# Seven block products for gate and up of the last 1024 tokens, in a one-core transformer layer

## The chip, the core and the metric

One NeuronCore of one Trainium2 chip runs the whole layer in one launch. The metric is device time in microseconds (us), the median of several executions. Engines are named as in the profile: PE is TensorE (PEld its weight loads), DVE is VectorE, ACT is ScalarE, POOL is GpSimd, SP is SyncE, whose queue issues all DMAs of this kernel.

## What is computed

One layer over 2048 tokens of 1024 features: three attention-like mixers, an output projection, then a gated feed-forward network with 2816 hidden features. The change touches the last of these:

```python
x = x + jnp.concatenate([out_a, out_b, out_c], axis=-1) @ w_out[l]
h = rms_norm(x, norm_ffn[l])
x = x + (jax.nn.silu(h @ w_ffn_gate[l]) * (h @ w_ffn_up[l])) @ w_ffn_down[l]
return rms_norm(x, final_norm)
```

All is float32. The kernel keeps each operand as a high part `hi` (the value rounded to fp32r) and a low part `lo = x - hi`, and makes each product of three matmuls: hi·hi, lo·hi and hi·lo.

## The kernel before

Tokens lie along the free axis in four groups of 512. A *tile* is 128 partitions by 512 float32. The program has two stages.

The **merged stage** runs two threads against each other (`merge`): the dense one (input projections, the two linear mixers, then the feed-forward network of token groups 0 and 1, one group at a time) and the sparse attention of all 16 query blocks. It lasts to the end of the last attention block. Weights are split into `hi` and `lo` once there (`load_halves`: ACT makes `hi`, L116, POOL makes `lo`, L119) and stored to DRAM as 512 KB tiles of both halves.

The **last stage** is `ffn([2, 3], ...)` for the last 1024 tokens, as two halves of 512. It loads the 512 KB tiles back (L131) and has these parts:

- The output projection: 8 output tiles times 2 halves times 8 contraction tiles times 3 matmuls (L175 to L177), with a residual add and squares for the norm. `n_lead = 6` output tiles start on contraction tiles 2 to 7 (`others`), since tiles 0 and 1 (`sparse`) come from the sparse attention.
- `normed(i)` per half: one matmul with ones (L202), rstd on ACT (L148, L149), then per contraction tile the scaled token tile on DVE (L229), `hi` on ACT (L231) and `lo` on DVE or POOL in turn (L232).
- For each pair of hidden tiles f, f+1: `gate_up(f)` and `gate_up(f + 1)` (L175 to L177; tanh on ACT L277, products on DVE L278 and L283, split on ACT and POOL L116, L119), then `down` of the pair before (L299 to L302).
- The tail: `down` of the last pair, norm, scaling, output (L326, L329).

The order is that of a scheduler which places the recorded instructions on each engine; a tile's buffers come free with the last use of the tile that held them. The pools of the last stage lie over the memory of those before, so that a load into them can wait for an older tile's last reader.

Of the kernel before, what the change touches and what calls it, by code (L numbers as in the profile page):

```python
# [75 lines left out]
SPEED = 1.3  # L76
FINE = 4

N_RAW, N_W, N_ACT = 3, 5, 3
A_RAW, A_W = 3, 5  # L80
N_GEN, N_MIX, N_ATT, N_NEAR = 4, 3, 3, 2

# [2 lines left out]
def hybrid_encoder_kernel(ctx, tc, xT, w_in, w_out, w_g, w_u, w_d, vec, wuk, wuv, wg2,  # L85
# [18 lines left out]
    cs = const.tile([P, C_SWA], F32, name="cs")  # L104
    vc = const.tile([P, NV], F32, name="vc")
    nc.sync.dma_start(out=vc, in_=vec)
    ident = cs[:, C_ID:C_ID + P]
# [34 lines left out]
    def store_halves():  # L142
        dst, w = unstored.pop(0)
        nc.sync.dma_start(out=dst, in_=w.bitcast(F32))

    def rstd_of(ss, n, dst):
# [10 lines left out]
        A.activation(dst, dst, AF.Exp)  # L157


    def ffn(groups, pools, ps_f, ps_n, n_raw, n_w, n_act, n_lead, before):  # L160

        fx, ft, fh, fl, fo, fs, fr = pools
        nh = len(groups)
        W = nh * 512
        halves = [slice(i * 512, (i + 1) * 512) for i in range(nh)]

        def load_w(src, f, c):
# [13 lines left out]

        sparse, others = range(2), range(2, KC)

        def operand(i, k):
            pool = fo if k in others else fs
            return (pool.tile([P, 512], F32R, tag=f"ah{k}{i}", bufs=1, name="ah"),
                    pool.tile([P, 512], F32R, tag=f"al{k}{i}", bufs=1, name="al"))

        def square(hs, k):

            if k == 0:
                A.activation(rs[:, hs], x2[:, k, hs], AF.Square)
            else:
                sq = fr.tile([P, 512], F32, tag="m", bufs=3, name="sq")
# [11 lines left out]

        def mixed(i, k):
            hi, lo = mixo[i][k]
            m = fr.tile([P, 512], F32, tag="m", bufs=3, name="m")
# [10 lines left out]
        def normed(i):  # L220

            hs = halves[i]
            norm_scale(hs)
            h2.append([])
            for k in range(KC):
                h2[i].append(operand(i, k))
                hi, lo = h2[i][k]
                hf = fr.tile([P, 512], F32, tag="m", bufs=3, name="hf")
# [4 lines left out]
                yield 0.4  # L233

        for k in others:
            mixed(0, k)
# [3 lines left out]
        for i, hs in enumerate(halves):  # L240
            lead = []
            for oc in range(KC):
                w = [load_w(w_out, oc, c) for c in range(2)]
                ps = ps_f()
                yield from product(ps, w, mixo[i], others, last=False)
                lead.append((oc, ps, w))
                yield 3.9 - 0.65 * (KC - FINE)
                if i == 0 and oc < n_lead - 1:
                    continue
                if i == 0 and oc == n_lead - 1:  # L250
                    yield from before
# [12 lines left out]
            yield from normed(i)  # L264

        def gate_up(f):
            ah = ft.tile([P, W], F32R, tag="fh", bufs=n_act, name="fh")
# [4 lines left out]
            for i, hs in enumerate(halves):  # L272
# [4 lines left out]
                A.activation(s, pg, AF.Tanh, scale=0.5)  # L277
                V.scalar_tensor_tensor(out=s, in0=s, scalar=1.0, in1=pg, op0=ALU.add, op1=ALU.mult)  # L278
                yield 5.2 - 0.65 * (KC - FINE)
                pu = ps_f()  # L280
# [4 lines left out]
                yield 5.2 - 0.65 * (KC - FINE)  # L285

        def down(fs, parts, last=False):

            n, ws = len(fs), {}
            for i2, hs in parts:  # L290
                if i2 not in ws:
                    ws[i2] = [load_w(w_d, f, i2) for f in fs]
# [58 lines left out]
    with ExitStack() as mx:  # L351
# [45 lines left out]
        def big():  # L397
            return bigp.tile([P, S], F32, tag="big", name="big")

        wuk_s = const.tile([P, 4, P], F32, name="wuk_s")  # L400
        wuv_s = const.tile([P, 256], F32, name="wuv_s")
        bits = const.tile([P, 32], I32, name="bits")

        def constants():
            nc.sync.dma_start(out=cs, in_=cst[:, 0:C_SWA])
# [713 lines left out]
        def dense():  # L1119
# [9 lines left out]
            with ExitStack() as f1:  # L1129
                fo, fr, fw, fx, ft = [f1.enter_context(tc.tile_pool(name=n, bufs=2))  # L1130
                                      for n in ("f1o", "f1r", "f1w", "f1x", "f1t")]
                pools = fx, ft, fw, fw, fo, fo, fr
                mf = f1.enter_context(tc.tile_pool(name="mf", bufs=3, space=PSUM))
                end = iter(())
                for g in range(2):
                    while len(attended) < 4 * g + 4:
                        yield None
                    end = yield from ffn([g], pools, lambda: mf.tile([P, 512], F32, tag="mf", name="mf"), ps_tr,
                                         N_RAW, N_W, N_ACT, 2, end)
                yield from end  # L1140

        drive(merge((dense(), NG * (PASS1 + PASS2) + 2 * FFN1),
# [1 line left out]

    with ExitStack() as f2:

        fx, ft, fo, fr, fh, fs, fl = [f2.enter_context(tc.tile_pool(name=n, bufs=2))
                                      for n in ("f2x", "f2t", "f2o", "f2r", "f2h", "f2s", "f2l")]
        pools = fx, ft, fh, fl, fo, fs, fr
# [98 lines left out]
```

## Time and profile before

| | us |
|---|---|
| runs | 2954.04, 2942.41, 2954.8; median 2954.04 |
| profiled execution, its own time | 2950.48 |
| its span | 2948.7 |
| merged stage, to the first matmul of the last stage | 2103.6 |
| output projection of the last 1024 tokens | to about 2201.5 |
| gate, up and down of 11 pairs | to about 2915 |
| end | 2948.7 |

The span is what the instruction rows cover; the execution's own time has 1.8 us more around it. The granted TensorE clock, as a mean over the span, is 0.973 of full speed. In rows of the timeline, a column in brackets is the engine's idle time just before, and what released it; `x12` means that so many instructions were put together.

### The profile page before, as it was taken

The numbers are of one execution on the slowest core, as the hardware profiler recorded it, in microseconds if no ns is written. First come the engines' busy times: TensorE is split into PE (matmuls) and PEld (weight loads), VectorE is DVE, ScalarE is ACT, GpSimd is POOL, SyncE is SP. The second block draws the span as 40 slices with busy tenths as digits, with TensorE's granted clock in tenths as the row PEclk, the third lists the DMA queues.
The fourth block names the chain that finished last, engine by engine and source line by source line (L and its number), as shares of the span: only waits on it lengthen the run. The fifth ranks groups of instructions, "written<-read, shape, count | busy, mean of one in ns | idle before, by whom it ended". The sixth has DMA issues, their size and how long they took to land.

```text
span 2948.7 us, 36635 instructions
## 1 busy us (share of the span) xinstructions
PE 2761.6 (94%) x13372; PEld 2171.4 (74%) x13372; DVE 1677.2 (57%) x3567; ACT 1181.1 (40%) x2061; POOL 582.8 (20%) x497
## 2 busy tenths in 40 slices
PE   7898999999999899999989999999899999999997
PEld 5666767676776767777767777777677888888886
DVE  3787887788767867475576673673342222222226
ACT  4655664665546655354553431441341000000004
POOL 3113420010100544444431100001111000000002
PEclk9998999999999989999999999999999999999998
DMA  7665534243332756666655444444572323323222
GB/s 248 193 190 191 183 122 142 92 149 106 103 128 78 268 179 229 227 214 225 226 187 193 142 150 143 137 152 147 188 249 87 108 92 100 100 86 107 93 93 72
DMA packets 179300, 451.12 MB, mean 153 GB/s; under 512 B 18632, under 2 KB 50288, under 8 KB 179120
## 3 DMA queue, kind: packets, MB, share of 16 engines
q1 hardware_dynamic: 179120, 448.78, 46.1%
q8 instruction: 105, 1.72, 0.2%
q14 instruction: 75, 0.61, 0.1%
HBM read 325.88 MB, written 122.83 MB: 152 GB/s over the span
## 4 chain that ended last, share of the span: by engine, by line
PE 59%; DVE 19%; ACT 8%; issue 7%; DMA 4%; POOL 2%; SPq 0%; DVEq 0%; ACTq 0%; POOLq 0%
PE pf L175 6%; PE pf L177 6%; PE pf L176 6%; DVE jd L937 6%; ACT jd L935 4%; PE mf L177 4%; PE mf L175 4%; PE mf L176 4%; PE pf L301 2%; PE pf L300 2%; PE pf L299 2%; PE mm L507 2%; PE mm L506 2%; PE mm L508 2%; PE mf L299 2%
## 5 line engine op out<-in xcount | busy, mean ns | idle before, releaser
L935 ACT ACTIVATE jd<-x,c 128x384 bf16<-128x384 f32 (+13 forms) x224 | 292.8, 1307 | 288.5 <-DVE c L962 228.7
L177 PE MATMUL mf<-al,w 128*128 128x512 f32 x832 | 329.1, 396 | 8.3 <-DVE al L212 4.1
L175 PE MATMUL mf<-ah,w 128*128 128x512 f32 x832 | 331.5, 399 | 3.7 <-ACT ah L231 2.8
L937 DVE TENSOR_SCALAR_CACHE_REDUCE jd<-x,c 128x384 bf16<-128x384 f32 (+13 forms) x224 | 330.9, 1477 | 6.5 <-DVE c L946 0.5
L175 PE MATMUL pf<-ah,w 128*128 128x512 f32 x832 | 325.1, 391 | 6.2 <-DMA w<-w 4.5
L119 POOL TENSOR_TENSOR w<-raw,w 128x512 fp32r<-128x512 f32 x192 | 260.0, 1362 | 341.4 <-ACT w L116 297.0
L176 PE MATMUL mf<-ah,w 128*128 128x512 f32 x832 | 327.4, 395 | 0.0
L177 PE MATMUL pf<-al,w 128*128 128x512 f32 x832 | 324.8, 391 | 1.3 <-POOL al L212 0.6
L176 PE MATMUL pf<-ah,w 128*128 128x512 f32 x832 | 325.3, 391 | 0.0
L119 POOL TENSOR_TENSOR fl<-u,fh 128x512 fp32r<-128x512 f32 x88 | 114.2, 1298 | 948.5 <-ACT fh L116 948.4
L506 PE MATMUL mm<-hh,w 128*128 128x512 f32 x576 | 241.3, 419 | 4.3 <-issue 2.0
L507 PE MATMUL mm<-hh,w 128*128 128x512 f32 x576 | 232.2, 403 | 0.6 <-POOL w L119 0.6
L508 PE MATMUL mm<-hl,w 128*128 128x512 f32 x576 | 230.9, 401 | 0.0
L177 PEld LDWEIGHTS mf<-al,w 128*128 128x128 f32 x832 | 158.5, 191 | 46.4 <-DVE al L212 4.5
L175 PEld LDWEIGHTS mf<-ah,w 128*128 128x128 f32 x832 | 159.0, 191 | 38.4 <-ACT ah L231 3.4
L175 PEld LDWEIGHTS pf<-ah,w 128*128 128x128 f32 x832 | 156.9, 189 | 39.9 <-DMA w<-w 4.9
L302 DVE TENSOR_TENSOR x<-x,pf 128x512 f32<-128x512 f32 (+1 forms) x184 | 121.9, 663 | 110.3 <-PE pf L301 110.0
L177 PEld LDWEIGHTS pf<-al,w 128*128 128x128 f32 x832 | 156.8, 188 | 35.9 <-POOL al L212 1.0
L176 PEld LDWEIGHTS mf<-ah,w 128*128 128x128 f32 x832 | 158.5, 190 | 31.7
L176 PEld LDWEIGHTS pf<-ah,w 128*128 128x128 f32 x832 | 156.8, 188 | 32.8 <-issue 0.5
L116 ACT CAST fh<-u 128x512 fp32r<-128x512 f32 x88 | 54.6, 620 | 308.1 <-DVE u L283 307.6
L299 PE MATMUL mf<-fh,w 128*128 128x512 f32 x352 | 147.0, 418 | 32.7 <-DVE x L302 17.3
(256 smaller groups left out, 5473.1 us busy)
## 6 DMA issues: line engine op xcount, KB each, us to landing
w<-w SPq DMA_DIRECT2D x636, 512.0 KB, 3.5
xk<-in_xT_dram SPq DMA_DIRECT2D x64, 256.0 KB, 3.3
raw<-in_w_in_dram SPq DMA_DIRECT2D x44, 256.0 KB, 3.7
raw<-in_w_g_dram SPq DMA_DIRECT2D x44, 256.0 KB, 3.7
raw<-in_w_u_dram SPq DMA_DIRECT2D x44, 256.0 KB, 3.9
raw<-in_w_d_dram SPq DMA_DIRECT2D x44, 256.0 KB, 4.3
m<-mixT SPq DMA_DIRECT2D x32, 256.0 KB, 3.1
x<-in_xT_dram SPq DMA_DIRECT2D x32, 256.0 KB, 4.6
```

Source lines behind the costliest of these rows:

```text
L119: Q.tensor_sub(lo, src, hi.bitcast(F32))
L175: T.matmul(ps, a, act[k][0], start=(first and k == ks[0]), stop=False)
L176: T.matmul(ps, b, act[k][0], start=False, stop=False)
L177: T.matmul(ps, a, act[k][1], start=False, stop=(last and k == ks[-1]))
L299: T.matmul(ps, hi[:, os_], ah[:, hs], start=(j == 0), stop=False)
L300: T.matmul(ps, lo[:, os_], ah[:, hs], start=False, stop=False)
L302: V.tensor_add(x2[:, oc, hs], x2[:, oc, hs], ps)
L506: T.matmul(ps, a, hh, start=(k == 0), stop=False)
L507: T.matmul(ps, b, hh, start=False, stop=False)
L508: T.matmul(ps, a, hl, start=False, stop=(k == KC - 1))
L935: A.activation(jd, xs, AF.Sign, scale=-1.0, bias=c[:, 0:1], accum_out=cnt)
L937: V.tensor_scalar(out=jd, in0=xs, scalar1=c[:, 0:1], scalar2=0.0, op0=ALU.is_ge, op1=ALU.add, accum_out=cnt)
```

## The change

Gate and up of the last 1024 tokens are cut into blocks: 2 hidden tiles (f, f+1), 2 halves of the contraction (4 tiles each), 2 halves of the tokens. Eight block products of 12 matmuls become seven, of sums of weight blocks (`s1` to `s4`) with sums of token blocks (`t1` to `t4`), as in Winograd's form of Strassen's scheme:

- `second_halves` makes the token sums, in the place of `normed` for the second half; `first_halves` keeps the scaled tiles of the first half (`kept`) for it.
- `quad` runs seven products of one weight matrix for one pair and puts them together on DVE, `take_gate` and `take_up` finish them. `first_quads` does gate and up of pair 0 while the token sums are made: six products run side by side, one contraction tile at a time.
- `summed` loads four raw weight blocks (L151, 256 KB each) and makes four sums on POOL (L153 to L156), `split` makes their halves on ACT and POOL (L114, L117). For pair 0 this runs in the merged stage (`summed_halves`, called from `gate_up` of group 1) and the halves go to DRAM; for the ten later pairs it runs in the last stage, one side ahead (`in_order`, `next_w`).
- The weight buffers of the last stage go from 9 to 6, temporaries from 3 to 7, raw tiles from 3 to 4 (in the merged stage too). Its pools are ordered anew, and four constants leave `const` for `pers`, which makes room.
- Per pair the order is gate, `down` of the pair before, up, where it was gate/up of f, gate/up of f+1, `down`.

```diff
-N_RAW, N_W, N_ACT = 3, 5, 3
+N_RAW, N_W, N_ACT = 4, 5, 3
...
+    def summed(src, f, pool, n_raw):
+        a = {}
+        for r in range(2):
+            for i in range(2):
+                a[r, i] = pool.tile([P, 512], F32, tag="raw", bufs=n_raw, name="raw")
+                nc.sync.dma_start(out=a[r, i], in_=src[f + r][:, i * 512:(i + 1) * 512])
+        s1, s2, s3, s4 = a[1, 1], a[0, 0], a[1, 0], a[0, 1]
+        Q.tensor_add(s1, a[1, 0], a[1, 1])
+        Q.tensor_sub(s3, a[0, 0], a[1, 0])
+        Q.tensor_sub(s2, s1, a[0, 0])
+        Q.tensor_sub(s4, a[0, 1], s2)
...
+        def second_halves():
+            norm_scale(halves[1])
+            for k in range(4):
+                b12, b22, t1, t2, t3, t4 = (temp() for _ in range(6))
+                scaled(k, 1, b12)
+                scaled(k + 4, 1, b22)
+                V.tensor_sub(t1, b12, kept[k])
+                hb["t1"].append(both(16 + k, t1, Q))
+                V.tensor_sub(t2, b22, t1)
+                hb["t2"].append(both(24 + k, t2, V))
+                V.tensor_sub(t3, b22, b12)
+                hb["t3"].append(both(8 + k, t3, Q))
+                V.tensor_sub(t4, kept[k + 4], t2)
+                hb["t4"].append(both(20 + k, t4, Q))
+                hb["b22"].append(both(12 + k, b22, V))
+                yield
...
+        def seventh(w, b):
+            ps = ps_f()
+            for k in range(4):
+                part(ps, w, hb[b][k], k, k == 0, k == 3)
+            return ps
...
         for f in range(0, NF, 2):
-            yield from gate_up(f)
-            if f and n_act < 4:
+            if nh == 1:
+                yield from gate_up(f)
+                if f:
+                    yield from down([f - 2, f - 1], steps)
+                yield from gate_up(f + 1)
+            elif f == 0:
+                yield from first_quads()
+            else:
+                yield from quad(w_g, f, take_gate)
                 yield from down([f - 2, f - 1], steps)
-            yield from gate_up(f + 1)
-            if f and n_act >= 4:
-                yield from down([f - 2, f - 1], steps)
+                room(f)
+                yield from quad(w_u, f, take_up)
...
-        fx, ft, fo, fr, fh, fs, fl = [f2.enter_context(tc.tile_pool(name=n, bufs=2))
-                                      for n in ("f2x", "f2t", "f2o", "f2r", "f2h", "f2s", "f2l")]
+        fx, ft, fs, fo, fr, fh, fb = [f2.enter_context(tc.tile_pool(name=n, bufs=2))
+                                      for n in ("f2x", "f2t", "f2s", "f2o", "f2r", "f2h", "f2b")]
...
-                                 lambda: pr.tile([P, 512], F32, tag="pm", name="pm"), 3, 9, 4, 6, iter(()))
+                                 lambda: pr.tile([P, 512], F32, tag="pm", name="pm"), 4, 6, 4, 6, iter(()))
```

Where instructions come to stand, at three places. First SP's queue at the seam of the two stages, before (`m` are mixer outputs for the projection, `out_dram` is the output of group 1, `w` the weight tiles, `mixT3<-ma` the last attention result):

```order
L210 DMA m_18214<-mixT2_60 128x512
L210 DMA m_18218<-mixT2_60 128x512
L210 DMA m_18222<-mixT2_60 128x512
L329 DMA out_0_dram<-x2_14013 128x2x512 x4
L131 DMA w_18238<-w44_9098 128x1024
L210 DMA m_18226<-mixT2_60 128x512
L210 DMA m_18230<-mixT2_60 128x512
L1088 DMA mixT3_61<-ma_18144 128x2x128
L210 DMA m_18234<-mixT2_60 128x512
L131 DMA w_18240<-w45_9104 128x1024
```

and now, behind seven `m` loads and four `raw` loads that stand just ahead of this piece:

```order
L129 DMA w_18302<-w44_9098 128x1024
L129 DMA w_18304<-w45_9104 128x1024
L129 DMA w_18325<-w46_9132 128x1024
L129 DMA w_18327<-w47_9139 128x1024
L539 DMA out_0_dram<-x2_14013 128x2x512 x4
L129 DMA w_18348<-w48_9221 128x1024
L129 DMA w_18350<-w49_9228 128x1024
L241 DMA m_18446<-mixT2_60 128x512
L247 DMA x2_18441<-in_xT_dram 128x512
L1306 DMA mixT3_61<-ma_18208 128x2x128
L247 DMA x2_18441<-in_xT_dram 128x512 x4
L129 DMA w_18371<-w50_9271 128x1024
```

The first four weight tiles now stand ahead of the output of group 1, and the first of them no longer waits for that output to land; the seventh weight tile waits for one of six buffers.

Second PE's queue where the second half's norm begins, before (`pm` is the matmul with ones, `pf_18934` the first gate product):

```order
L177 MATMUL pf_18934<-al_18567,w_18926 128x512
L175 MATMUL pf_18934<-ah_18572,w_18926 128x512
L202 MATMUL pm_18872<-rs_18376,ones_85 128x512
L176 MATMUL pf_18934<-ah_18572,w_18926 128x512
L177 MATMUL pf_18934<-al_18573,w_18926 128x512
```

and now (`pf_18956` is the second block product, `pf_19013` the third):

```order
L353 MATMUL pf_18956<-ah_18638,w_18954 128x512
L354 MATMUL pf_18956<-al_18639,w_18954 128x512
L233 MATMUL pm_18974<-rs_18440,ones_84 128x512
L352 MATMUL pf_19013<-ah_18644,w_19011 128x512
L353 MATMUL pf_19013<-ah_18644,w_19011 128x512
```

`pm` stood behind 10 matmuls of the stretch that follows the output projection; it stands behind 24 now. Behind it come 24 more that need the first half alone, and then 72 that need token sums.

Third DVE's queue in the same stretch, before (`hf` are scaled tiles, `al` low parts, `s` is a gate):

```order
L229 SCALAR_TENSOR_TENSOR hf_18878<-x2_18377,vc_83,rs_18376 128x512
L229 SCALAR_TENSOR_TENSOR hf_18884<-x2_18377,vc_83,rs_18376 128x512
L229 SCALAR_TENSOR_TENSOR hf_18890<-x2_18377,vc_83,rs_18376 128x512
L229 SCALAR_TENSOR_TENSOR hf_18896<-x2_18377,vc_83,rs_18376 128x512
L232 TENSOR_TENSOR al_18883<-hf_18884,ah_18882 128x512
L229 SCALAR_TENSOR_TENSOR hf_18902<-x2_18377,vc_83,rs_18376 128x512
L278 SCALAR_TENSOR_TENSOR s_18959<-s_18959,pf_18934 128x512
```

and now, for the first of four contraction tiles (`t_18980` to `t_18983` are `t1` to `t4`):

```order
L271 SCALAR_TENSOR_TENSOR t_18978<-x2_18441,vc_82,rs_18440 128x512
L271 SCALAR_TENSOR_TENSOR t_18979<-x2_18441,vc_82,rs_18440 128x512
L300 TENSOR_TENSOR t_18980<-t_18978,hf_18618 128x512
L302 TENSOR_TENSOR t_18981<-t_18979,t_18980 128x512
L304 TENSOR_TENSOR t_18982<-t_18979,t_18978 128x512
L306 TENSOR_TENSOR t_18983<-hf_18642,t_18981 128x512
L277 TENSOR_TENSOR al_18993<-t_18981,ah_18992 128x512
L277 TENSOR_TENSOR al_19007<-t_18979,ah_19006 128x512
```

Twelve DVE instructions for the second half become 32, eight per contraction tile; POOL has three low parts per tile beside them, 12 where it had four.

## Rows read from the trace of the kernel before

**Rows 1.** The page: busy time of the engines, and slices of the span.
```profile
span 2948.7 us, 36635 instructions
...
PE 2761.6 (94%) x13372; PEld 2171.4 (74%) x13372; DVE 1677.2 (57%) x3567; ACT 1181.1 (40%) x2061; POOL 582.8 (20%) x497
...
PE   7898999999999899999989999999899999999997
...
PEclk9998999999999989999999999999999999999998
```

**Rows 2.** Busy time by stretch: us, busy of each engine, clock, DMA share, GB/s.
```profile
1600.00:2080.00 480.00, 454.86 (x2248) 366.25 (x2247) 272.85 (x501) 165.75 (x220) 39.83 (x37) 0.98 0.44 141
2103.00:2204.00 101.00, 94.19 (x397) 75.91 (x398) 37.34 (x51) 27.88 (x43) 15.34 (x11) 0.97 0.82 282
2300.00:2900.00 600.00, 600.00 (x2649) 496.99 (x2648) 154.77 (x226) 43.91 (x72) 46.48 (x36) 1.00 0.29 94
```

**Rows 3.** The page's costliest groups: block matmuls (L176, L177 have as many).
```profile
L175 PE MATMUL pf<-ah,w 128*128 128x512 f32 x832 | 325.1, 391 | 6.2 <-DMA w<-w 4.5
```

**Rows 4.** The timeline of PE at the seam of the stages.
```profile
2103.57 0.47 PE L175 MATMUL pf<-ah,w 128*128 128x512 f32 x1 [1.03 <-DVE ma L1087]
...
2109.71 0.80 PE L175 MATMUL pf<-ah,w 128*128 128x512 f32 x1 [4.52 <-DMA w<-w]
...
2114.97 0.39 PE L175 MATMUL pf<-ah,w 128*128 128x512 f32 x1
```

**Rows 5.** The timeline of SP's queue at the seam.
```profile
2090.80 5.05 SPq L329 DMA_DIRECT2D out_dram<-x  x4
2099.50 0.34 SPq L131 DMA_DIRECT2D w<-w  x1
...
2104.67 18.98 SPq L131 DMA_DIRECT2D w<-w  x11
```

**Rows 6.** Busy time by stretch, after PE's idle time at the seam.
```profile
2110.00:2115.00 5.00, 5.00 (x13) 3.91 (x13) 0.00 (x0) 0.00 (x0) 0.00 (x0) 0.51 1.02 419
2115.00:2120.00 5.00, 5.00 (x24) 4.14 (x23) 0.00 (x0) 0.00 (x0) 0.00 (x0) 1.00 0.83 329
```

**Rows 7.** The timeline of the second half's norm, PE and DVE.
```profile
2203.74 1.12 PE L202 MATMUL pm<-rs,ones 128*128 128x512 f32 x2
...
2207.57 2.08 DVE L229 SCALAR_TENSOR_TENSOR hf<-x,vc,rs 128x512 f32<-128x512 f32 x3 [3.89 <-ACT rs L149]
...
2219.34 1.18 DVE L232 TENSOR_TENSOR al<-hf,ah 128x512 fp32r<-128x512 f32 x1
```

**Rows 8.** One line's instructions: ns min/median/max, of DVE and POOL.
```profile
L229 DVE SCALAR_TENSOR_TENSOR hf<-x,vc,rs x32: 739/746/1781, 1040.3 to 2217.5; 128x512 f32<-128x512 f32 x32
L232 DVE TENSOR_TENSOR al<-hf,ah x16: 675/680/1753, 1045.2 to 2219.3; 128x512 fp32r<-128x512 f32 x16
```

**Rows 9.** Groups by line and shape: operations on POOL, DVE and ACT.
```profile
L119 POOL TENSOR_TENSOR fl<-u,fh 128x512 fp32r<-128x512 f32 x88 | 114.2, 1298 | 948.5 <-ACT fh L116 948.4
L302 DVE TENSOR_TENSOR x<-x,pf 128x512 f32<-128x512 f32 x168 | 115.5, 687 | 109.4 <-PE pf L301 109.1
L116 ACT CAST fh<-u 128x512 fp32r<-128x512 f32 x88 | 54.6, 620 | 308.1 <-DVE u L283 307.6
```

**Rows 10.** The page's DMA issues: KB each, us from issue to landing.
```profile
w<-w SPq DMA_DIRECT2D x636, 512.0 KB, 3.5
raw<-in_w_u_dram SPq DMA_DIRECT2D x44, 256.0 KB, 3.9
```

**Rows 11.** What PE waited for: first 2195 to 2230 us, last row 2230 to the end.
```profile
PE pf L175 <- ACT ah L231: 0.7, 1, 0.7
PE pf L177 <- DVE al L232: 0.5, 1, 0.5
PE pf L177 <- POOL al L232: 0.2, 1, 0.2
...
PE pm L202 <- DVE rs L197: 11.3, 2, 6.5
```

More of the change, by code (lines that the diff above doesn't have):

```diff
@@ L233, in normed, with temp, scaled, both @@
                 yield 0.4
+        def temp():
+            return fr.tile([P, 512], F32, tag="m", bufs=n_m, name="t")
+        def scaled(k, i, dst):
+            V.scalar_tensor_tensor(out=dst, in0=x2[:, k, halves[i]], scalar=vc[:, V_FFN + k:V_FFN + k + 1],
+                                   in1=rs[:, halves[i]], op0=ALU.mult, op1=ALU.mult)
+        def both(j, x, eng):
+            hi, lo = pair(j)
+            A.copy(hi, x)
+            eng.tensor_sub(lo, x, hi.bitcast(F32))
+            return hi, lo
@@ new lines, in ffn, with first_halves @@
+        hb = {n: [] for n in ("b11", "b21", "b22", "t1", "t2", "t3", "t4")}
+        kept = []
+        def first_halves():
+            norm_scale(halves[0])
+            for k in range(KC):
+                kept.append(fb.tile([P, 512], F32, tag=f"b{16 + k}l", bufs=1, name="hf"))
+                scaled(k, 0, kept[k])
+                hb["b11" if k < 4 else "b21"].append(both(k, kept[k], V if k % 2 else Q))
+                yield 0.4
+        def second_halves():
[13 more added lines that the diff above has]
+                hb["b22"].append(both(12 + k, b22, V))
+                yield
@@ new lines, in weight, with in_order @@
+        def weight(src, f, a):
+            r, i = {"a11": (0, 0), "a12": (0, 1), "a22": (1, 1)}.get(a, (0, a))
+            return load_halves((src.tensor.name, f + r, i), None, None, 0, fh, n_w)
+        ORDER = "a11", "s2", "s3", "s1", "a12", "s4", "a22"
+        sums = {}
+        def in_order():
+            for f in range(2, NF, 2):
+                for src in (w_g, w_u):
+                    for a in ORDER:
+                        if a in sums:
+                            w = fh.tile([P, 1024], F32R, tag="w", bufs=n_w, name="w")
+                            hi, lo = w[:, 0:512], w[:, 512:1024]
+                            split(sums[a], hi, lo)
+                            yield hi, lo
+                        else:
+                            if a == "a11" and f == 2 and src is w_g:
+                                sums.update(summed(src, f, fr, n_raw))
+                            yield weight(src, f, a)
+                        if a == "s4" and (src is w_g or f + 2 < NF):
+                            sums.update(summed(*((w_u, f) if src is w_g else (w_g, f + 2)), fr, n_raw))
+                    if src is w_g:
+                        yield from (load_w(w_d, f - 2 + j, i2) for i2 in range(2) for j in range(2))
+            yield from (load_w(w_d, NF - 2 + j, i2) for i2 in range(2) for j in range(2))
@@ new lines, in ffn, with next_w, part @@
+        coming, ready = in_order(), []
+        def next_w(ahead=3):
+            while len(ready) <= ahead:
+                w = next(coming, None)
+                if w is None:
+                    break
+                ready.append(w)
+            return ready.pop(0)
+        def part(ps, w, b, k, first, last):
+            hi, lo = w
+            x, y = (t[:, k * P:(k + 1) * P] for t in (hi, lo))
+            T.matmul(ps, x, b[0], start=first, stop=False)
+            T.matmul(ps, y, b[0], start=False, stop=False)
+            T.matmul(ps, x, b[1], start=False, stop=last)
@@ new lines, in ends_of, with first_quads @@
+        def ends_of(src, f, take, u4, u3):
+            w4, w22 = (weight(src, f, a) for a in ("s4", "a22")) if f == 0 else (next_w(), next_w())
+            V.tensor_add(u4, u4, seventh(w4, "b22"))
+            take(f, 0, 1, u4)
+            yield 2.7
+            V.tensor_add(u3, u3, seventh(w22, "t4"))
+            take(f, 1, 0, u3)
+            yield 2.7
+        def first_quads():
+            sides = ((w_g, take_gate), (w_u, take_up))
+            p1 = [ft.tile([P, 512], F32, tag="p1", bufs=2, name="p1") for _ in sides]
+            for x, (src, _) in zip(p1, sides):
+                A.copy(x, seventh(weight(src, 0, "a11"), "b11"))
+            room(0)
+            tokens = second_halves()
+            next(tokens)
+            for x, (src, take) in zip(p1, sides):
+                c11 = temp()
+                V.tensor_add(c11, x, seventh(weight(src, 0, "a12"), "b21"))
+                take(0, 0, 0, c11)
+            ws = [[(b, weight(src, 0, a)) for b, a in (("t1", "s1"), ("t2", "s2"), ("t3", "s3"))] for src, _ in sides]
+            ps = [[ps_f() for _ in w] for w in ws]
+            for k in range(4):
+                for pp_, w_ in zip(ps, ws):
+                    for p_, (b, w) in zip(pp_, w_):
+                        part(p_, w, hb[b][k], k, k == 0, k == 3)
+                next(tokens, None)
+                yield 4.1
+            for (src, take), (p5, p6, p7), x in zip(sides, ps, p1):
+                u2, u3, c22 = temp(), temp(), temp()
+                V.tensor_add(u2, x, p6)
+                V.tensor_add(u3, u2, p7)
+                V.tensor_add(c22, u3, p5)
+                V.tensor_add(u2, u2, p5)
+                take(0, 1, 1, c22)
+                yield from ends_of(src, 0, take, u2, u3)
@@ L263, in ffn @@
                     yield 1.3
-            yield from normed(i)
+            yield from normed(i) if nh == 1 else first_halves() if i == 0 else iter(())
         def gate_up(f):
@@ L279, in gate_up @@
                 yield 5.2 - 0.65 * (KC - FINE)
+                next(prepare, None)
                 pu = ps_f()
@@ L285, in gate_up @@
                 yield 5.2 - 0.65 * (KC - FINE)
+                next(prepare, None)
         def down(fs, parts, last=False):
```

78 lines of the change are left out of this document (64 added, 14 removed).

## The prediction

> **What bounds the kernel now.** I read the page first. PE is busy 94% of the span, and hardly a slice is under eight tenths [rows 1]. Then the busy time by stretch [rows 2]: from 2300 to 2900 us PE is busy 600.0 of 600 us at clock 1.00, so there the number of matmuls is the time: 600 / 2649 = 0.2265 us each. (A record of one lasts 391 ns [rows 3], since matmuls overlap; the count in a stretch gives the price, not the mean.) DVE, ACT and POOL are busy 155, 44 and 46 us of those 600, and DMA has a share of 0.29. In the merged stage's last 480 us PE is busy 455, and POOL 40. In the output projection PE is busy 94 of 101 us. So the last stage pays for each matmul, save at its seams: where it begins [rows 4 to 6], where the second half's norm is made [rows 7, 11], and at the end.
>
> **(a) Matmuls removed.** Gate and up of the last 1024 tokens have 22 hidden tiles x 2 halves x 8 contraction tiles x 3 matmuls x 2 matrices = 2112. Seven block products in place of eight leave 1848, so 264 fewer; the orders show 3600 and 3336 block matmuls in the last stage. All stand where PE never idles: 264 x 0.2265 = **-59.8 us** [rows 2].
>
> **The steady stretch has room for what is added.** A pair now costs PE 14 products x 12 x 0.2265 = 38.0 us, and `down` 96 x 0.2265 = 21.7: 59.7 us. Beside it POOL has 8 sums, 8 splits and 4 low parts, 20 x 1.3 = 26 us; DVE some 38 x 0.69 = 26; ACT some 20 x 0.62 = 12.5 [rows 9]. DMA moves some 7 MB per pair, 117 GB/s where it now moves 94 [rows 2], and 282 in the projection. None is near 59.7 us. The tightest chain is the sums for a gate behind an up: the four buffers come free with the split of `s4` (0.62 + 1.3, some wait with it: 2.2), the load takes 3.9 [rows 10], four sums 5.2, a split 1.9: 13.2 us. The next `a11` and the products behind give it 8 products, 21.7 us; 8.5 are left. The sums of an up behind a gate have `down` as well, 21 us more. I cost these at nothing; POOL and DVE hide under PE, and if a chain is over its cover PE waits for the difference at each of 10 sides.
>
> **(b) The seam.** Before, PE waits 4.52 us for the second weight tile [rows 4]. On SP's queue the weight loads stand behind the output of group 1: four issues from 2090.80, the first weight at 2099.50, eleven more from 2104.67 over 18.98 us [rows 5]. After the wait 12 matmuls go from 2109.71 to 2114.97 us, 5.26 for 2.7: about half the clock, though the five-us row that straddles its return says 1.02, and from 2115 it is 24 matmuls in 5 us [rows 4, 6]. In the changed order four weight tiles stand ahead of the output and the first does not wait for it. That would return 4.52 + 2.6 = 7.1. The 1.03 us wait for the attention result stays. With six buffers in place of nine some loads of the projection come tighter: the second tile of output tile 4 is issued 18 matmuls (4.1 us) ahead, a landing takes 3.5 [rows 10]; I give 1 us back. **-6.0**, bounds -7.1 and 0.
>
> **(c) The token sums, the dear part.** Count from the last projection matmul. 24 matmuls (5.4 us), `pm` of two matmuls (1.1), 24 more (5.4): 12.0 us of work that needs no token sum; then 72 that need them, 16.3, together 28.3 without waits. The first scaled tile of the second half comes 3.8 us behind `pm`'s start, 2203.74 to 2207.57 [rows 7]: at 5.4 + 3.8 = 9.2. Then DVE has eight instructions per contraction tile, four tiles, all in one row, and PE's matmuls follow tile by tile. Four additions that put `c11` together (2.75 us) stand between the first and second tile; the last tile's eighth instruction (0.7) lies beside matmuls, and 10 matmuls follow it.
> - Low end: DVE as when alone, 2 x 0.746 + 6 x 0.68 = 5.6 per tile [rows 8, 9]; POOL's 3 x 1.3 = 3.9 lies beside it. 9.2 + 22.4 + 2.75 - 0.7 + 2.3 = 36.0: PE waits 7.7. Before, it lost 0.7 + 0.5 + 0.2 = 1.4 at this place [rows 11], so **+6.3**.
> - High end: DVE stands still during each POOL instruction, 5.6 + 3.9 = 9.5 per tile, and the last ten matmuls go at half clock (4.4, by the 12 of [rows 4]): 9.2 + 38 + 2.75 - 0.7 + 4.4 = 53.6, **+23.9**.
> - Taken: the nearest row is the second half's norm as it is now, where POOL has low parts too. There 12 DVE instructions and two of a gate last from 2207.57 to 2220.52; less 1.36 for the two, 11.6 us, where alone they need 8 x 0.746 + 4 x 0.68 = 8.7 [rows 7, 8]. That is 0.97 each, 7.8 per tile: 9.2 + 31.2 + 2.75 - 0.7 + 3.3 (between both clocks) = 45.8. PE waits 17.5 us, **+16.2** with the 1.4 taken off.
>
> These same rows show a maximum of 1781 and 1753 ns for an instruction that mostly takes 746 and 680 [rows 8]: about one POOL instruction (1298 [rows 9]) longer. The Trainium skill, "SBUF — State Buffer", section "Who interferes with whom", states that a VectorE instruction with two SBUF inputs and a GpSimd one that reads SBUF share a port pair, and that whoever comes second is blocked for the other's whole instruction. That speaks against this change, which makes five of six sums and all low parts in SBUF on these two engines at once; by the rule alone the high end of (c) would hold, and the sum below would be -36.7 in place of -44.4.
>
> **(d)** The weight tile of gate's `s4` for pair 0 is issued some 12 matmuls (2.7 us) ahead, and lands in 3.5 [rows 10]: **+1**, between 0 and 3.
>
> **(e) The end.** The last block product put together belongs to the first half's tokens of the pair whose `down` is the tail. Two DVE instructions 0.69 each, ACT 0.62, POOL 1.3: 3.3 us [rows 9] against 10 matmuls (2.3) that are scheduled ahead of its reader: **+1.2**, between 0 and 3. The tail's norm keeps its 6.5 us wait [rows 11].
>
> **(f) The merged stage** gets eight sums and eight splits more on POOL (16 x 1.3 = 21 us), eight copies on ACT (5), eight loads of 256 KB, eight stores. POOL has 440 us idle of 480 [rows 2], but PE is at 455 of 480, and what comes late there is paid at once: **+3**, bounds 0 and half of POOL's 21, 10.
>
> **Sum.** -59.8 - 6.0 + 16.2 + 1.0 + 1.2 + 3.0 = -44.4. The profiled execution has 2950.5 us (its span 2948.7), so 2906.1; the median of the runs is 3.6 above the profiled execution: rounded down a little, **2908 us**. All low ends give -60.6 (2893 by the median), all high ends -19.9 (2934).
>
> **Rivals.**
> 1. *VectorE is not held up by GpSimd here.* For it: most L229 and L232 records have the lone duration [rows 8], and the scheduler may set POOL's parts into gaps. Against it: the 0.97 us of [rows 7]. Then (c) is +6.3, the sum -54.3: some 2899 us. Chance 0.17.
> 2. *The stretch is worse than the nearest row*: full blocking, PE at half clock behind each wait, and merged-stage work late as well. For it: 1.7 us maxima, and PE's 12 matmuls at half speed behind a single wait [rows 4, 8]. Against it: POOL's three low parts per tile come when DVE has eight, so they need not all meet. (c) +23.9 and (f) up to +10: 2915 to 2931. Chance 0.08.
> 3. *Six weight buffers are too few for the projection.* It streams 8 MB in 101 us at 282 GB/s, DMA share 0.82 [rows 2]; its loads then wait for a buffer and not only for the queue. At 1 us on each of 26 loads behind the sixth buffer, +26 in place of the +1 in (b): -19.4, some 2935 us, within half a per cent of 2954. For it: PE waits 6.2 us for weights in all already [rows 3]. Against it: each 512 KB tile feeds 24 matmuls, 5.4 us, and lands in 3.5. Chance 0.05.
> 4. *The other side: the sums of weights come late in every side.* Place: the ten up-to-gate passages of the steady stretch, where `summed` waits for four raw buffers. To be slower by 0.5%, the change must lose 44.4 + 14.8 = 59 us, 5.9 per passage; with its margin of 8.5 the chain of 13.2 would have to last 27.6 us, twice as long. That needs POOL's nine instructions in it to be held up by DVE for some 1.6 us each, or stand behind others in POOL's row. For it: a POOL row of 20 per pair, all with SBUF on both sides, beside 26 us of DVE. Against it: 26 of 59.7 us are little, and most L302 additions read a PSUM bank. Then some 2969 us or more. Chance 0.04.
>
> That the change does not do what it says is excluded by the order: the 264 matmuls are gone.
>
> **The numbers.** The forecast's own mechanism has 0.66, rivals 1 to 4 have 0.17, 0.08, 0.05 and 0.04. What a measurement here can tell from no change is about 0.5%, 14.8 us, so faster means under 2939.2. Forecast and rivals 1 and 2 are faster: 0.91. Rival 3 is mostly the same: 0.05. Rival 4 is slower: 0.04. The range goes from 2886 (the low ends, 2893, and half of the 12 us by which the runs of before differ) to 2934 (all high ends).
>
> **What the profile afterwards should show.** L352 to L354 with 616 matmuls each, and 0.2265 us a matmul in the steady stretch at clock 1.00, with no waits per pair; POOL some 26 us in 60 there. At the seam the 4.52 us wait gone. In the 45 us behind the projection PE waits of `pf` for `al` from DVE and POOL, 17.5 us together; under 10 would make rival 1 right, over 22 rival 2. At most 2 us before the tail's first `down`. A wait of `pf` for `w` in the projection over 10 us would be rival 3, one for `hi` or `lo` of sums once per pair rival 4. Wrong altogether would be a merged stage that ends more than 10 us later than 2103.6, or a PE busy time that falls by much less than 59.8.

## The result, and the profile after

The changed kernel takes 2915.39 us (median of 4 runs, 2914.02 to 2916.37), the one before 2952.45 us in the same comparison; the ratio is 0.9881, 95% interval 0.9863 to 0.9899. That is 1.2% faster, inside the predicted range and 7 us above the forecast. The profiled execution took 2915.7 us, its span is 2913.9.

The page of the changed kernel: span and busy time.

```profile
span 2913.9 us, 37130 instructions
...
PE 2714.8 (93%) x13108; PEld 2125.9 (73%) x13108; DVE 1838.8 (63%) x3741; ACT 1252.6 (43%) x2183; POOL 834.7 (29%) x681
...
L354 PE MATMUL pf<-al,w 128*128 128x512 f32 x616 | 242.3, 394 | 7.5 <-POOL al L277 3.9
```

PE has 264 matmuls less and POOL is busy 252 us more. The busy time by stretch (columns as in [rows 2]): the projection, the first products of pair 0, two pieces of the latter, and the steady stretch.

```profile
2116.00:2208.00 92.00, 89.56 (x387) 72.20 (x388) 39.95 (x48) 25.50 (x40) 16.95 (x11) 1.00 0.75 245
2208.00:2257.00 49.00, 36.93 (x127) 25.98 (x126) 39.53 (x41) 19.20 (x29) 22.20 (x13) 0.86 0.26 82
...
2225.00:2230.00 5.00, 5.00 (x12) 3.98 (x13) 4.73 (x7) 1.20 (x2) 1.00 (x1) 0.50 0.02 3
...
2235.00:2240.00 5.00, 4.41 (x10) 3.01 (x11) 5.00 (x5) 0.62 (x1) 3.22 (x2) 0.50 0.00 0
...
2300.00:2850.00 550.00, 550.00 (x2429) 455.40 (x2428) 255.16 (x349) 100.76 (x164) 243.23 (x181) 1.00 0.38 121
```

In the steady stretch 550 / 2429 = 0.2264 us a matmul, as in [rows 2]; POOL is busy 243 of 550 us, 26.4 in 59.7, as worked out. PE never waits there. Cut at four marks in PE's row (the first projection matmul, the first gate or up matmul, the 121st of these, the end), the two spans compare so:

| stretch | before, us | after, us | change | forecast |
|---|---|---|---|---|
| to the first projection matmul | 2103.57 | 2116.24 | +12.7 | +3 |
| projection | 97.77 | 91.65 | -6.1 | -6.0 |
| first 120 gate and up matmuls | 30.60 | 48.21 | +17.6 | +16.2 |
| from there to the end | 716.76 | 657.82 | -58.9 | -57.6 |
| span | 2948.7 | 2913.9 | -34.8 | -44.4 |

So three terms stand, and one, the merged stage, was priced too low. The line before the span has the 59.8 of (a) less 0.9 for (d) and (e): PE waits for no weight tile behind the projection, and from 2270 us on its only waits are these, two in the final norm, as before, and one for POOL:

```profile
PE pm L233 <- DVE rs L228: 11.1, 2, 6.2
PE pf L511 <- POOL fl L117: 0.6, 1, 0.6
```

### The profile page after: what moved, and what is told of

It reads as the page before. It is cut to its first block, busy times and chain, and to the rows that moved or that the text cites. A ratio compares the mean times of both kernels' runs of the same rounds, so it can differ in the third digit from the quotient of the medians.

```text
span 2913.9 us, 37130 instructions
## 1 busy us (share of the span) xinstructions
PE 2714.8 (93%) x13108; PEld 2125.9 (73%) x13108; DVE 1838.8 (63%) x3741; ACT 1252.6 (43%) x2183; POOL 834.7 (29%) x681
## 4 chain that ended last, share of the span: by engine, by line
PE 60%; DVE 21%; ACT 8%; issue 6%; DMA 3%; POOL 2%; SPq 0%; DVEq 0%; ACTq 0%; POOLq 0%
DVE jd L1155 6%; PE pf L354 5%; PE pf L353 5%; PE pf L352 5%; PE mf L201 4%; PE mf L199 4%; PE mf L200 4%; ACT jd L1153 4%; PE pf L511 3%; PE pf L510 3%; PE pf L509 3%; PE mm L725 2%; PE mm L724 2%; PE mm L726 2%; PE mf L509 2%
## 5 line engine op out<-in xcount | busy, mean ns | idle before, releaser
L117 POOL TENSOR_TENSOR w<-raw,w 128x512 fp32r<-128x512 f32 x272 | 366.9, 1358 | 611.5 <-ACT w L114 568.6
L199 PE MATMUL mf<-ah,w 128*128 128x512 f32 x832 | 332.1, 400 | 4.2 <-ACT ah L262 1.7
L114 ACT CAST w<-raw 128x512 fp32r<-128x512 f32 x272 | 165.4, 617 | 379.1 <-PE pf L511 191.1
L354 PE MATMUL pf<-al,w 128*128 128x512 f32 x616 | 242.3, 394 | 7.5 <-POOL al L277 3.9
L352 PE MATMUL pf<-ah,w 128*128 128x512 f32 x616 | 242.2, 393 | 4.6 <-ACT ah L276 4.6
L353 PE MATMUL pf<-ah,w 128*128 128x512 f32 x616 | 241.4, 392 | 0.0
L199 PEld LDWEIGHTS mf<-ah,w 128*128 128x128 f32 x832 | 159.2, 191 | 39.3 <-ACT ah L262 2.9
L117 POOL TENSOR_TENSOR fl<-u,fh 128x512 fp32r<-128x512 f32 x44 | 57.2, 1300 | 338.2 <-ACT fh L114 338.1
L512 DVE TENSOR_TENSOR x<-x,mf 128x512 f32<-128x512 f32 x176 | 118.8, 682 | 52.1 <-PE mf L511 51.8
L354 PEld LDWEIGHTS pf<-al,w 128*128 128x128 f32 x616 | 116.7, 190 | 35.5 <-DVE al L277 5.7
L511 PE MATMUL mf<-fl,w 128*128 128x512 f32 x352 | 140.9, 400 | 1.2 <-POOL fl L117 1.2
```

Of the source, the lines that this page charges most:

```text
L117: Q.tensor_sub(lo, src, hi.bitcast(F32))
L199: T.matmul(ps, a, act[k][0], start=(first and k == ks[0]), stop=False)
L352: T.matmul(ps, x, b[0], start=first, stop=False)
L353: T.matmul(ps, y, b[0], start=False, stop=False)
L354: T.matmul(ps, x, b[1], start=False, stop=last)
```

## The experiments

A ratio is that to the kernel before in the same comparison, with its 95% interval; a time without one is a single execution.

**Both kernels again**, unchanged, to see how far profiles of one kernel scatter.

> The kernel before, once more, for the scatter of the merged stage's end. It ended at 2103.57 us in the profile shown. If profiles of one kernel scatter by 1 to 2 us there, the 12.7 us by which the changed kernel reaches the last stage later (2116.24) are the change's; a scatter of 5 us or more would leave much of it unexplained.

> The changed kernel once more. Theory: the last stage begins at 2116 us again, within 2 us, the whole takes 2914 to 2917. Rival (scatter): the last stage begins more than 5 us earlier or later.

They took 2955.15 and 2914.74 us. The last stage began at 2106.01 and 2115.25 us. The scatter comes from the first third: the first matmul of the feed-forward row (L175, now L199, with output `mf`) starts between 971 and 981 us in the profiles of this study, whatever the kernel. Counted from that matmul, the rest of the merged stage takes 1127.5 us in both profiles of the kernel before, 1137.7 and 1139.7 in the changed one (and 1135.0, 1136.4 and 1138.0 in three later runs that leave this stage as the change has it). Of the 12.7 us, then, 7 to 12 are the change's, 10 in the mean, and the rest is scatter. This count, from that matmul to the first of the last stage, is used below.

**No sums for pair 0 in the merged stage**, with four and with three raw buffers. These kernels leave the sums out and load plain weight tiles in their place, as many.

```diff
-  summed_halves((w_g, w_u), fr, N_RAW, fw) if g else iter(())
+  iter(())
-  "a22": (1, 1)}.get(a, (0, a))
+  "a22": (1, 1)}.get(a, (0, 0))
```

and for the second, in addition:

```diff
-N_RAW, N_W, N_ACT = 4, 5, 3
+N_RAW, N_W, N_ACT = 3, 5, 3
```

> Left out: the weight sums of pair 0 in the merged stage (their loads, sums, splits and stores); the last stage loads a plain weight tile in the place of each of these sums. All else as in the changed kernel. Theory (the sums' copies stand in ACT's row ahead of attention's copies and wait there for POOL and for the one store buffer): the 8 us that are lost between 1575 and 1607 us come back, and some of the 5 before; the last stage begins at 2104 to 2109 us, the whole takes 2903 to 2908. Rival (the fourth raw buffer and the loads it lets ahead cost the 12.7 us, not the sums): the last stage still begins at 2113 or later, the whole takes 2912 or more.

> As the run without pair 0's sums in the merged stage, and the merged stage's raw tiles have three buffers again, as before the change. Theory: 0 to 3 us less than with four buffers, last stage from 2103 to 2107 us, the whole 2902 to 2907. Rival (the fourth buffer): 8 to 12 us less than with four buffers.

2903.33 us (ratio to before 0.9841, 0.9827 to 0.9856) and 2900.16 us (0.9829, 0.9813 to 0.9846). The theory: the count is 1127.8 in both, as before the change, so the sums cost the 10 us there and the fourth raw buffer nothing of them. In both the last stage begins somewhat earlier than expected, at 2102.93 and 2098.88 us. The 3 us between the two runs lie in the first third in the profiles, within its scatter; but the executions of the two kernels do not overlap, so a small share of the fourth buffer there is not excluded.

**Where do the sums cost it?** Most of it at the passage from group 1's attention to its feed-forward: 130 matmuls there take 31.8 us before and 39.8 after. ACT's and POOL's rows of the changed kernel there, and what PE waited for from 1560 to 1625 us:

```profile
1583.01 0.62 ACT L114 CAST ws<-raw 128x512 fp32r<-128x512 f32 x1 [4.72 <-DMA w<-ws]
...
1596.01 0.62 ACT L114 CAST ws<-raw 128x512 fp32r<-128x512 f32 x1 [3.83 <-POOL raw L153]
1596.53 0.58 ACT L1267 COPY pT<-tr 128x512 f32<-128x512 f32 x1
```
```profile
1594.71 1.26 POOL L153 TENSOR_TENSOR raw<-raw 128x512 f32<-128x512 f32 x1 [4.41 <-DMA raw<-in_w_u_dram]
```
```profile
PE o L1275 <- ACT pT L1267: 5.4, 2, 4.0
PE mf L201 <- DVE al L263: 1.4, 1, 1.4
...
PE mf L201 <- POOL al L263: 1.1, 2, 0.8
```

A copy for a weight sum waits 4.72 us until the one tile for split sums, `ws`, is stored. The next waits 3.83 us for POOL, whose sum waits for a raw tile, and attention's copy `pT` stands behind it; PE waits 4.0 us for that. After it PE has clock 0.50 from 1597 to 1602, where the kernel before has 1.00 over the matching matmuls (1587 to 1591):

```profile
1597.00:1602.00 5.00, 4.84 (x20) 3.61 (x21) 2.58 (x2) 2.05 (x5) 4.49 (x4) 0.50 0.17 71
```
```profile
1585.00:1590.00 5.00, 4.83 (x37) 3.37 (x33) 2.41 (x4) 2.82 (x5) 0.00 (x0) 1.00 0.64 196
```

Two runs try this. In the first, POOL makes the high parts:

```diff
-  split(x, w[:, 0:512], w[:, 512:1024])
+  split(x, w[:, 0:512], w[:, 512:1024], Q)
```

> The high parts of pair 0's eight weight sums are made by POOL in the merged stage, no longer by ACT; the loads, sums, low parts and stores stay. Theory (these copies stand in ACT's row ahead of attention's copies and wait there for sums and for the store buffer): most of the 12 us come back though all the work stays; the last stage begins at 2104 to 2109 us, the whole takes 2903 to 2909. Rival (the loads and stores on SP's queue, or POOL's own row, are late): the last stage begins at 2113 or later, the whole takes 2912 or more.

2909.39 us (0.9858, 0.9841 to 0.9874): between the two ranges, so neither theory nor rival. The count is 1134.5, just under the changed kernel's, and the 130 matmuls still take 38.1 us. The wait for `pT` is back to 1.5, but another has come, of PE for POOL's row:

```profile
PE mf L201 <- POOL al L263: 5.2, 2, 5.0
...
PE o L1275 <- ACT pT L1267: 1.5, 1, 1.5
```
```profile
1603.47 0.93 POOL L116 CAST ws<-raw 128x512 fp32r<-128x512 f32 x1 [1.02 <-DMA w<-ws]
1604.47 1.26 POOL L117 TENSOR_TENSOR ws<-raw,ws 128x512 fp32r<-128x512 f32 x1
1605.69 2.50 POOL L263 TENSOR_TENSOR al<-hf,ah 128x512 fp32r<-128x512 f32 x2
```

The stall moved to POOL's row, where the sums and their halves stand ahead of the low parts `al` of group 1's tokens. So it is not ACT's row alone. In the second run the work stays and the splits move behind that passage, from the one `ws` tile into the five weight buffers of group 1:

```diff
-  w = pool.tile([P, 1024], F32R, tag="ws", bufs=1, name="ws")
+  w = pool.tile([P, 1024], F32R, tag="w", bufs=N_W, name="ws")
...
-                next(prepare, None)
+                if f >= 4:
+                    next(prepare, None)
```

> Pair 0's weight sums are split later in the merged stage: their split tiles take turns in the five weight buffers of group 1's feed-forward, from its fifth hidden tile on, in place of a buffer of their own; all the work stays. In the order, ACT's eight copies now stand behind the casts of group 1's norm and not among attention's copies; POOL's first four sums stay where they were, the rest moves too. Theory (the price is the place, at group 1's seam, in ACT's and POOL's rows): the last stage begins at 2103 to 2107 us, the whole takes 2902 to 2907. Rival (the work itself costs it, wherever it stands): 2910 or more.

2900.06 us (0.9829, 0.9813 to 0.9845): the theory, 2 us under its range. The count is 1126.3, the 130 matmuls take 32.5 us, and PE's waits there, first block, are those of the kernel before, second block:

```profile
PE o L1277 <- ACT pT L1269: 1.4, 1, 1.4
...
PE mf L201 <- POOL al L263: 0.8, 1, 0.8
```
```profile
PE o L1057 <- ACT pT L1049: 1.4, 1, 1.4
...
PE mf L177 <- POOL al L232: 0.8, 1, 0.8
```

All eight sums, splits and stores are still made. So the price was not the work but where in the rows it stands and what it waits for there. The run changes two things, the place and the number of tiles for split sums; five tiles in the old place were not tried, so how much each returns is not shown. This version beats the changed kernel by some 15 us, 11 of them by the count.

**The token sums.** DVE's and POOL's rows of the changed kernel for the first contraction tile, and PE's waits behind the projection:

```profile
2218.17 1.41 DVE L271 SCALAR_TENSOR_TENSOR t<-x,vc,rs 128x512 f32<-128x512 f32 x2 [8.00 <-ACT rs L172]
...
2220.83 0.68 DVE L304 TENSOR_TENSOR t<-t 128x512 f32<-128x512 f32 x1
2221.43 1.76 DVE L306 TENSOR_TENSOR t<-hf,t 128x512 f32<-128x512 f32 x1
2223.11 3.44 DVE L277 TENSOR_TENSOR al<-t,ah 128x512 fp32r<-128x512 f32 x2
...
2220.98 5.02 POOL L277 TENSOR_TENSOR al<-t,ah 128x512 fp32r<-128x512 f32 x3 [39.76 <-ACT ah L276]
```
```profile
PE pf L352 <- ACT ah L276: 4.6, 3, 2.5
PE pf L354 <- POOL al L277: 3.9, 4, 1.1
PE pf L354 <- DVE al L277: 3.6, 4, 1.3
```

Three DVE instructions take 1.76, 1.72 and 1.72 us in place of 0.69 beside three of POOL, which take 1.67 in place of 1.30 [rows 8, 9]. A tile takes DVE 8.3 to 9.4 us. Two runs test this. The first kernel leaves out POOL's three low parts per tile, and the matmuls take the high part in their place (`t3` and `t4` like `t1`):

```diff
+        def alone(j, x):
+            hi, lo = pair(j)
+            A.copy(hi, x)
+            return hi, hi
...
-                hb["t1"].append(both(16 + k, t1, Q))
+                hb["t1"].append(alone(16 + k, t1))
```

> Left out: POOL's twelve low parts of token sums (t1, t3, t4) behind the projection; the matmuls take the high part in their place. Theory (DVE sets the pace there, and three of its eight instructions per tile are held up by POOL's, 1.75 us in place of 0.69): a tile takes 5.6 us of DVE in place of 8.4 to 9.5; the first 120 matmuls of pair 0 take 36 to 39 us in place of 48.2; the whole falls by 9 to 12, to 2903 to 2907. Rival (ACT's copies, or the order of the row, set the pace): they take 44 us or more, the whole falls by less than 4.

2904.24 us, and the first 120 matmuls take 36.87: the theory. DVE's third tile starts at 2231.59 and its fourth at 2236.72, 5.1 us apart:

```profile
2231.59 1.41 DVE L271 SCALAR_TENSOR_TENSOR t<-x,vc,rs 128x512 f32<-128x512 f32 x2
...
2235.52 1.28 DVE L277 TENSOR_TENSOR al<-t,ah 128x512 fp32r<-128x512 f32 x2
2236.72 1.40 DVE L271 SCALAR_TENSOR_TENSOR t<-x,vc,rs 128x512 f32<-128x512 f32 x2
```

So the low end of (c) is about what DVE does without POOL beside it. In the second run DVE makes these low parts itself (`t3` and `t4` likewise):

```diff
-  hb["t1"].append(both(16 + k, t1, Q))
+  hb["t1"].append(both(16 + k, t1, V))
```

> POOL's twelve low parts of token sums go to DVE, which has eleven instructions per tile then. Theory (an instruction of DVE that meets one of POOL's here waits for it, 1.75 us in place of 0.69, so that POOL's help costs more than it saves): a tile takes 2 x 0.75 + 9 x 0.68 = 7.6 us of DVE in place of 8.4 to 9.5; the first 120 matmuls of pair 0 take 44 to 46 us in place of 48.2, the whole 2910 to 2913. Rival (POOL's help is worth its price): 48 us or more, the whole 2914 or more.

2911.17 us, the first 120 matmuls in 42.91: the theory, and for these 1 us better than its low end. The prices left out that back-to-back instructions of DVE start 0.60 to 0.61 us apart, not 0.68. Three low parts in one row:

```profile
2239.40 1.89 DVE L277 TENSOR_TENSOR al<-t,ah 128x512 fp32r<-128x512 f32 x3
```

Eleven instructions of DVE are quicker here than eight beside three of POOL.

**The margin of the steady stretch.** Behind each weight sum of the ten later pairs POOL adds and subtracts the same tile once more.

```diff
+    def again(f, s, y):
+        if f:
+            Q.tensor_add(s, s, y)
+            Q.tensor_sub(s, s, y)
...
         Q.tensor_add(s1, a[1, 0], a[1, 1])
+        again(f, s1, a[1, 0])
```

(`s3`, `s2` and `s4` likewise.)

> In the last stage each weight sum is followed by an addition and a subtraction of the same tile on POOL, so that POOL has three instructions for each sum: 36 per pair and 20 sides in place of 20. Theory (the chain for a gate behind an up takes 13.2 us against 21.7 of cover): 8 x 1.3 = 10.4 us more make it 23.6, 1.9 too late at each of 10 sides: the whole takes some 2925 to 2945. Rival one (the cover is larger than I counted): no change, 2912 to 2918. Rival two (POOL's row as a whole is near its limit): 2950 or more.

2939.34 us, 24 more than the changed kernel's 2915: the theory. Behind the first 120 matmuls it takes 685.74 us in place of 657.82. PE's new waits:

```profile
PE pf L362 <- POOL w L117: 9.5, 9, 1.6
PE pf L361 <- DVE t L405: 7.1, 5, 1.5
PE pf L361 <- DMA w<-w: 5.9, 4, 1.8
```

They stand at nine of the ten up-to-gate passages and nowhere else, two at each, 22.5 / 9 = 2.5 us together where 1.9 was expected. The stretch lost 27.9 us, 3.1 at each, so the margin of 8.5 us was right to a microsecond or so. This is the fourth rival's wait, and it takes ten microseconds of POOL more in each chain to bring it about.

**The seam without the rest.** In the kernel before, the last stage's pools in another order:

```diff
-        fx, ft, fo, fr, fh, fs, fl = [f2.enter_context(tc.tile_pool(name=n, bufs=2))
-                                      for n in ("f2x", "f2t", "f2o", "f2r", "f2h", "f2s", "f2l")]
+        fx, ft, fr, fh, fo, fs, fl = [f2.enter_context(tc.tile_pool(name=n, bufs=2))
+                                      for n in ("f2x", "f2t", "f2r", "f2h", "f2o", "f2s", "f2l")]
```

> The kernel before with nothing changed but the order in which the last stage's pools are laid out, so that its weight tiles do not lie over group 1's output: eight weight loads and more stand ahead of the output's stores on SP's queue. Theory (the seam's share of the change comes from this alone): the 4.5 us wait and the half clock behind it go, the projection takes 91 to 92 us in place of 97.8, the whole 5 to 7 us less than before. Rival (it comes with the rest of the change, the traffic or the six buffers): the projection takes 96 us or more, the whole is the same within 2 us.

2947.39 us against 2949.94, ratio 0.9993 (0.9984 to 1.0001); the projection takes 95.65 us where the kernel before takes 97.77. The theory fails, and by a little the rival's bounds do too: 2 us come back, and no difference in the whole is shown. PE no longer waits for weights, but now the mixer outputs `m` are loaded late, behind group 1's output, and PE waits for their halves.

```profile
PE pf L175 <- ACT ah L211: 2.8, 3, 1.6
...
PE pf L177 <- POOL al L212: 1.4, 3, 0.6
```
```profile
2092.93 5.05 SPq L329 DMA_DIRECT2D out_dram<-x  x4
2102.33 1.29 SPq L210 DMA_DIRECT2D m<-mixT  x3
```

In the changed kernel seven `m` loads stand ahead of the output as well as four weight tiles. So the 6.1 us seem to need both; the `m` loads ahead without the weights were not tried, nor whether seven temporaries or the pool order put them there.

**Pair 0 with eight products.** If its early sums and its token wait cost more than 24 matmuls (5.4 us), plain products for this one pair should be better. Pair 0's weight sums leave the merged stage: `first_quads` makes them half by half, `second_halves` first splits the second half's own tiles and then makes `t1` to `t3`, a new `fourth_sums` makes `t4`. Nothing is left out; the lines below are the products.

```diff
+  for i in range(2):
+      for src, take in ((w_g, take_gate), (w_u, take_up)):
+          for r in range(2):
+              w = [load_w(src, r, c) for c in range(2)]
+              ps = ps_f()
+              yield from product(ps, w, hb["b11"] + hb["b21"] if i == 0 else hb["b12"] + hb["b22"])
+              take(0, r, i, ps)
...
+  fourth_sums()
```

> Pair 0 with eight block products as before the change (24 matmuls more), the ten later pairs with seven; pair 0's weight sums leave the merged stage; the token sums are made beside pair 0's matmuls: first the second half's own tiles, then t1 to t3, at the end t4. Nothing is left out. Theory: the merged stage ends 12 us earlier, pair 0 takes 192 x 0.2265 + 0.9 = 44.4 us, with 0 to 3 of waits, in place of 59.1: together 24 to 27 us less, 2888 to 2892. Rival (the token sums now come late for pair 1, whose first sum is needed 2.7 us behind pair 0): waits of 5 to 15 us there, 2895 to 2906.

2899.09 us (0.9827, 0.9810 to 0.9845): the rival. Pair 0 takes 44.4 us without a wait and the merged stage's count is 1127.6, both as expected. But 11 us are lost behind it, where PE waits in pair 1's gate:

```profile
PE pf L366 <- POOL al L277: 4.5, 3, 2.4
PE pf L364 <- DMA w<-w: 1.8, 1, 1.8
```

The first line is the low parts of `t4`. In the next run pair 0's `down`, with its weight loads, stands ahead of that gate:

```diff
+  if f == 2:
+      yield from down([0, 1], steps)
   yield from quad(w_g, f, take_gate)
-  yield from down([f - 2, f - 1], steps)
+  if f > 2:
+      yield from down([f - 2, f - 1], steps)
```

> As the run with eight block products for pair 0, and pair 0's down stands ahead of pair 1's gate, so that the token sums have 21.7 us more. Nothing is left out. Theory (the 11.2 us that were left behind pair 0 are waits for t4 and the half clock behind them): they go, the whole takes 2885 to 2890. Rival (DVE and POOL are so far behind that the sums of weights for pair 1 come late too): 2893 to 2900.

2901.41 us (0.9834, 0.9821 to 0.9847): 1 us beyond even the rival's range, and no better than the run before. The waits for `t4` are gone; PE waits in `down` instead, for low parts in POOL's row and for additions in DVE's:

```profile
PE pf L512 <- POOL fl L117: 3.4, 2, 2.4
PE pf L510 <- DVE x L513: 3.3, 1, 3.3
```

It looks as if the two engines are behind as a whole, and it matters little which of their results PE asks for next. Eight products for pair 0 beat the changed kernel by some 16 us, but are not clearly better than seven with the splits moved, 2900.06.

## Why the prediction was right, and where not

The mechanism holds: fewer matmuls where PE never idles, paid for in part where the token sums are made. In spans the forecast missed 9.6 us, and nearly all of that is the merged stage, (f).

- **(a)** holds to the rounding: 264 matmuls at 0.2264 us, and no wait in the steady stretch. PE's busy time falls by 46.8 us and not by 59.8, which was a sign for "wrong altogether". Behind the first 120 gate and up matmuls it falls by 59.3, so the matmuls are gone as forecast. Ahead of that, PE is busy longer with as many matmuls: 6.9 us in the first 120, where half the clock is granted for a while, and 5.6 in all that stands before.
- **(b)** has the right size, -6.1 for -6.0. SP's queue shows it: four weight tiles and then the output, and PE's first wait is again of 1.03 us, though now put down to POOL and not to the attention result.

```profile
2095.37 1.75 SPq L129 DMA_DIRECT2D w<-w  x4
2103.50 5.05 SPq L539 DMA_DIRECT2D out_dram<-x  x4
```
```profile
2116.24 0.47 PE L199 MATMUL pf<-ah,w 128*128 128x512 f32 x1 [1.03 <-POOL al L243]
```

  Its reason was half of it: the weights' place alone returns 2 us or so, as the run with the other pool order shows. The prediction also misread a row of [rows 6]: the 1.02 is the DMA share, and the clock there is 0.51, which bears its half clock out. Rival 3, six buffers too few, is out: PE waits 1.1 us for weights in the projection.
- **(c)** was +16.2 and is +17.6. The mechanism, DVE held up by POOL, is shown by the two runs on it; that the total is so close is in part luck. The first scaled tile came at 10.3 us and not at 9.2, because ACT's copy of a block product stands ahead of the norm's table load, which before was done when `pm` ended. The four tiles took DVE 34.5 us and not 31.2, 8.6 each for 7.8. The 0.97 us per instruction from [rows 7] had a wrong reading in it, too: 1.19 of the 2.9 us lost there were a wait of DVE for POOL, seen in the kernel before:

```profile
2210.84 1.76 DVE L229 SCALAR_TENSOR_TENSOR hf<-x,vc,rs 128x512 f32<-128x512 f32 x1 [1.19 <-POOL al L232]
```

  Against these 4.4 us, the last matmuls came 2.0 us sooner behind the last tile than forecast, and the kernel before lost some 1 us more than the 1.4 taken off.
- **The signs for (c)** were badly chosen: PE's waits are 12.1 us, not 17.5, yet the 120 matmuls take 20.1 us more than the 28.1 without waits (pair 0 with eight products). The half clock, 0.50 from 2225 to 2230 and again from 2235 to 2240, makes up some 5, and starting anew behind each of eleven waits the rest.
- **(d), (e)** were 2.2 and are 0.9.
- **(f)** is the step that failed: "PE is at 455 of 480, and what comes late there is paid at once: +3, bounds 0 and half of POOL's 21, 10". By the count it is 7 to 12, 10 in the mean, at its upper bound, and makes the forecast 7 us too low; scatter of the first third adds 2.5 in the profiles shown. The sign "ends more than 10 us later" came, with 12.7. I priced the work and read POOL's idle time in the stage's last 480 us. The sums stand earlier, from 1515 us on, and at the one passage where ACT and POOL both serve attention and the norm; there an instruction that waits for a raw tile or a store holds up those behind it. The run that moves them, and gives them more tiles, shows that the same work costs nothing elsewhere.
- **Rival 1** (no hold-up) is out. Of **rival 2**, late work in the merged stage came true, and 2915 is the lower edge of its 2915 to 2931; but not its full blocking: DVE lost 1.07 us at a meeting where a POOL instruction takes 1.30, and the half clock came behind some waits only. The sum by the high end of (c), -36.7, comes near the measured -37.1 for another reason: the loss is in (f).
- **Rival 4** needed twice the chain; tripled sums, not the change, bring its wait about.

Two sums of the rivals do not come out: rival 2's terms end at some 2924, not 2931, and rival 3's 2935 is 0.66% under 2954, not within half a per cent. (c) as taken gives +16.1, not +16.2.

## What to carry to other kernels

An idle engine hides work only where its row has no one waiting behind it: ask not how busy POOL and ACT are, but which of their next instructions PE needs, and what the added ones wait for. Two engines that hold each other up, as DVE and POOL do here, are to be counted as nearly one: giving the idle one a share can cost more than doing it all on the other. Where the start of a stage is stalled by loads, see that all its first operands come ahead of the stores; in the run that moved the weights alone, the wait only changed its name.

## What the runs showed of the hardware

- DVE and POOL hold each other up where each reads two SBUF tiles: DVE takes 1.72 to 1.76 us for 0.69, POOL 1.67 to 1.73 for 1.30. The Trainium skill, "SBUF — State Buffer", section "Who interferes with whom", has the loser blocked for the other's whole instruction. The trace agrees in kind; in size DVE lost 1.07 us at a meeting, less than POOL's 1.30, POOL lost 0.4 too, and in most tiles only three of eight DVE instructions met one. Moving the work back to DVE pays: 42.9 us for 48.2.
- Short waits in a row can go with the half clock: PE waited 1.05, 1.07 and 1.15 us between 2219.8 and 2224.9 us; the granted clock was 0.84 from 2220 to 2225 and 0.50 from 2225 to 2230, and 12 matmuls from 2224.93 on took 0.44 us each. With the five waits of 0.60 to 1.26 us between 2242 and 2254 the clock was 1.00 from 2245 on. In all, the 12.1 us of waits in (c) cost 20.1.
